# A hybrid GLA and gated-DeltaNet block on one core: where the scores, the gate and ScalarE's weight splits stand in the program order of the GDN heads

## The chip, the core and the metric

The kernel runs on one core of one Trainium2 chip. The metric is the device time of one execution in microseconds (us), lower is better; the median of three runs is given for the kernel before. Besides the times there is a profile: one execution recorded instruction by instruction.

## What is computed

One layer, 1024 tokens of width 1024, in fp32. Cut to what matters:

```python
h = rms_norm(x, pre_mix_w) * (1.0 + scale1) + shift1
proj = h @ w_in                              # q, k, v, g, ... of both branches
o_a = gla_chunked(a_q, a_k, a_v, a_gk)       # 4 heads, gated linear attention
y_a = (rms_norm(o_a, gla_onorm_w) * silu(a_g)) @ w_branch_gla
d_qkv = silu(causal_short_conv(d_qkv, gdn_conv_w))          # 4 taps
o_d = gated_delta_chunked(l2_norm(d_q), l2_norm(d_k), d_v, beta, g)   # 8 heads
y_d = (rms_norm(o_d, gdn_onorm_w) * silu(d_g)) @ w_branch_gdn
merged = sigmoid(m_a) * y_a + sigmoid(m_d) * y_d
x = x + gate1 * rms_norm(merged @ w_out, post_mix_w)
y = square(relu(h2 @ mlp_w1)) @ mlp_w2       # h2: x normed and modulated again
x = x + gate2 * rms_norm(y, post_mlp_w)
```

Inside a GDN head, over chunks of tokens: `att = q k^T * decay`, then, chunk by chunk, `v_new = u - w S`, `o = q_dec S + att v_new`, `S = dec * S + k_state^T v_new`.

## The kernel before

**Matmuls.** An fp32 operand is kept as two fp32r tiles, a rounded high part and the remainder (`hH`, `hL` of the activations, `wH`, `wL` of the weights, `oH`, `oL` of a branch's output), and a product is the sum of three: high by high, low by high, high by low. `dense_b` makes one 128x1024 tile of a projection in PSUM: eight k-steps of six matmuls of 128x512 (`dense_k`), with `tick()` behind each. Two such tiles fit in PSUM at a time (pool `pm`); the small products share four half-size buffers (`pa`).

**What sets the order.** Work beside the dense tiles is put on an agenda by step: `at(dt, fn)` means dt steps from now, and in a head `on(t, fn)` means step t of that head, counted from its first k-step. `tick()` calls what is due. While the GDN heads run, and up to the fifth tile behind them, each of TensorE, VectorE and ScalarE issues in the order in which the program was written (`InOrder` with `strict`), so the agenda is the order of each queue: an instruction that isn't ready holds everything behind it on its engine. The DMA queue of SyncE isn't held to this, and loads are issued ahead.

**A GDN head** (`gdn_head`) spans three dense tiles, 24 steps: psq (steps 0 to 7), psv (8 to 15), psg (16 to 23), for q, v and the gate g. q goes through `conv_silu` during psv: a copy and three shifted multiply-adds (`cv` with `pm`), tanh on ScalarE (`si`), and a last multiply on VectorE (`cv<-si,cv`), after which q is whole. Then `att(0)` and `att(1)` make the scores on TensorE, four matmuls of 128x128 each (`pa<-cv,kT`), and VectorE multiplies them by the decays (`attT<-pa,Dt`). `eg` (the exponential of the gates, later multiplied by q to `qd`) and `ke` (k by a decay) are loaded over all partitions from `gc_d` and `ner_d` and finished on VectorE.

The head's chain of eight chunks follows at its steps 24 to 47, in the first two tiles of the next head (head 7's in the first two tiles of the branch matmul): every three steps `c0` (transpose of v and `st,ke`, then `rs` on ScalarE), `c1` (`pa<-rs,U`, then `vn` on ScalarE) and `c2` (`vn,kt`, `vn,attT`, `st,eg`, then the new state `st` on VectorE). After the fourth and the eighth chunk ScalarE squares and copies the outputs (`ob`, `so`). At step 48 `norm` runs 14 small instructions on VectorE (a reciprocal root by Newton steps, `rsqrt`), at 50 `scale`, at 52 and 53 `fin` transposes, and the result is multiplied by the gate and stored.

The gate is made by `silu_twice(psg)`, right behind psg's last step: tanh on ScalarE (`si<-pm`) and two halves on VectorE (`si<-si,pm`). That place, where one head ends and the next begins, is called the border here.

**The branch matmul.** Behind head 7 `dense_n` makes eight tiles of o_a by `w_branch_gla`, here oa0 to oa7, and eight more by `w_branch_gdn`. The operand o_a is loaded, cast and split tile by tile (`Split`: `load`, `high` on ScalarE, `low` on VectorE) at the steps of three tables at the end of head 7. The weights are split by `conv_w_tile`: `wH` is cast on ScalarE, `wL` is written there as the negated weight, rounded the same way, and a DMA issued from GpSimd adds the whole weight onto it from DRAM, which leaves the remainder and spends no time of VectorE. `next_w` fetches the split of the next tile while the current one runs; before, both ScalarE instructions are issued at once, at the tile's start. VectorE also sums rows of the conditioning matrix (`aacc`, `ada_sum`), one every 13 steps.

In the profile nearly every instruction has line 38, that of the recording helper; they are told apart by their tiles.

Of the kernel before, what the change touches and what calls it, by code (L numbers as in the profile page):

```python
# [8 lines left out]
F32 = mybir.dt.float32  # L9
# [41 lines left out]
def block_kernel(ctx: ExitStack, tc: tile.TileContext, x, c, ada_w, ada_b, pre_mix_w, post_mix_w,  # L51
# [332 lines left out]
    plan += [(w_in, c0 + h * 128, 128, 8, E) for h in range(8) for c0, E in ((C_DQ, (1, 5) if h else (4, 6)), (C_DV, (1, 3)), (C_DG, (1, 4)))]  # L384
    plan += [(w, j * 256, 256, 8, None) for w in (w_bgla, w_bgdn) for j in range(4)]

    def conv_w_later(raw_ap, shape, dh, dl):

        w = [None, None]

        def high():
            w[0] = t4(shape, F32R, "wH", "wt")
            A.copy(w[0], raw_ap)

        def low():
            w[1] = t4(shape, F32R, "wL", "wt")
            V.tensor_tensor(w[1], raw_ap, w[0].bitcast(F32), ALU.subtract)

        at(dh, high)
        at(dl, low)  # L400
        return w

    def splits():
        early = {}

        def load(e):
            early[e] = load_raw(*plan[e][:3])

        first = next(e for e, p_ in enumerate(plan) if type(p_[4]) is tuple)
        for e, (w, c0, n, kt, E) in enumerate(plan):  # L410
            raw = early.pop(e) if e > first else load_raw(w, c0, n)
            if type(E) is tuple:
                at(E[1] + 1, lambda: load(e + 1))
                yield conv_w_later(raw, (128, 8, 128), *E)
            elif kt == 4:
                yield [conv_w_tile(raw[:, 4 * i:4 * i + 4, :], (128, 4, 256), E=E) for i in range(2)]
            else:
                for i in range(n // 128):
                    c1 = c0 + i * 128
                    src = None if E else w[:, c1:c1 + 128].rearrange("(k p) c -> p k c", p=128)  # L420
# [354 lines left out]
    def gdn_head(h):  # L775
# [3 lines left out]
        def on(t, fn):  # L779
            at(begin + t - clock[0], fn)  # L780
# [105 lines left out]
        qd = eg  # L886
        if h == 7:
            for k in range(8):
                on((8, 9, 10, 11, 18, 18, 19, 20)[k], lambda k=k: oa_s.load(k))
                on(18 + k, lambda k=k: oa_s.high(k))  # L890
                on((19, 21, 22, 23, 25, 26, 27, 29)[k], lambda k=k: oa_s.low(k))
# [34 lines left out]
        def c2(t):  # L926
# [26 lines left out]

# [7 lines left out]
        def fin(hf):  # L961
            pt, h_ = pat(), slice(hf * 512, (hf + 1) * 512)
            for i in range(4):
                t = hf * 4 + i
                T.transpose(pt[:, i * 128:(i + 1) * 128], c["ob"][:, t * 128:(t + 1) * 128], ident)
            on(53 + hf, lambda: V.scalar_tensor_tensor(sg[:, h_], pt, don, sg[:, h_], ALU.mult, ALU.mult))
            if hf:
                on(56, lambda: A.dma_start(od_d[h], sg))
# [12 lines left out]
        sg = silu_twice(psg)  # L981


    smask = [None]
# [917 lines left out]
    fin = {}  # L1902
# [72 lines left out]
```

## Time and profile before

| | |
|---|---|
| median of three runs | 1965.05 us (1964.96 to 1965.36) |
| the profiled execution's own time | 1965.17 us |
| its span | 1963.4 us, 25782 instructions |
| mean granted TensorE clock | 0.990 |
| granted clock by slices | 8 tenths in the first of 40 slices, 9 or more in all others |
| HBM traffic | 220.14 MB read, 75.15 MB written, 150 GB/s over the span |

A timeline row gives the start in us, the duration (of a group: from its first start to its last end), the engine, the operation, the tile written and the tiles read, the count, and in brackets how long the engine stood idle before it, with what ended the idle time. A windows row gives for a stretch of time each engine's busy time, then the granted clock, the DMA engines' mean share and their GB/s. A waits row gives the idle time in us, the number of waits and the longest. Durations of matmuls overlap, since they are pipelined.

### The profile page before, as it was taken

Reading aid. Unit: us, or ns where it says so; the run is one execution under the profiler, and the core shown is the slowest. Engines: PE = TensorE matmul, PEld = TensorE weight load, DVE = VectorE, ACT = ScalarE, POOL = GpSimd, SP = SyncE. Lnnn points to the kernel's source line nnn. Section 1 sums busy time; section 2 is a strip of 40 time slices with the busy share of each in tenths; the row PEclk is TensorE's granted clock in tenths of the full one; section 3 lists DMA queues with packets and bytes.
Section 4 is the critical chain, followed back from the end, with each engine's and each line's share of the span. In section 5 each row is a group of like instructions: output and inputs, shape, how many; then the busy total and the mean of one; then the engine's idle time right before and its main releaser. Section 6 shows DMA issues by size and latency. Waiting matters only on the chain.

```text
span 1963.4 us, 25782 instructions
## 1 busy us (share of the span) xinstructions
PE 1913.2 (97%) x9847; PEld 1610.1 (82%) x9847; DVE 1367.0 (70%) x2454; ACT 819.1 (42%) x1483; POOL 171.3 (9%) x120
## 2 busy tenths in 40 slices
PE   5999999999999999999999999999999999999998
PEld 4778888889899888888887888888888888888886
DVE  7866599758768556666666234666668886787887
ACT  5545322342342344444445331247644446343333
POOL 3400100310101100000000110000012220000001
PEclk8999999999999999999999999999999999999999
DMA  9355631423122434444456895244666767452525
GB/s 296 110 203 176 207 104 69 161 65 107 55 76 65 144 112 128 128 128 128 128 180 170 192 216 120 106 129 161 203 213 215 248 225 256 162 204 63 205 97 97
DMA packets 217850, 296.96 MB, mean 151 GB/s; under 512 B 36016, under 2 KB 156351, under 8 KB 217727
## 3 DMA queue, kind: packets, MB, share of 16 engines
q1 hardware_dynamic: 178238, 248.22, 39.2%
q10 hardware_dynamic: 21840, 35.04, 4.8%
q0 software_dynamic: 17648, 12.06, 4.6%
q8 instruction: 77, 1.26, 0.3%
q14 instruction: 47, 0.38, 0.1%
HBM read 220.14 MB, written 75.15 MB: 150 GB/s over the span
## 4 chain that ended last, share of the span: by engine, by line
PE 93%; DVE 2%; DMA 2%; ACT 1%; issue 1%; SPq 1%; DVEq 0%; ACTq 0%
PE pm L38 62%; PE pa L38 31%; DMA araw<-in_ada_w_dram 1%; DVE acc L38 1%; DVE cv L38 1%; DMA gr<-gc_d 1%; DMA x<-in_x_dram 0%; DVE gr L38 0%; DVE lba L38 0%; SPq L227 0%; SPq L220 0%; ACT ktok L38 0%; ACT oH L38 0%; DVE ya L38 0%; DVE rt L38 0%
## 5 line engine op out<-in xcount | busy, mean ns | idle before, releaser
L38 PE MATMUL pm<-hH,wH 128*128 128x512 f32 x1008 | 330.3, 409 | 3.8 <-DVE cv L38 3.8
L38 PE MATMUL pm<-hL,wH 128*128 128x512 f32 x1008 | 314.3, 392 | 0.0
L38 PE MATMUL pm<-hH,wL 128*128 128x512 f32 x1008 | 312.5, 391 | 0.1
L38 PEld LDWEIGHTS pm<-hH,wL 128*128 128x128 f32 x1008 | 189.4, 188 | 42.2 <-DVE wL L38 0.5
L38 PEld LDWEIGHTS pm<-hL,wH 128*128 128x128 f32 x1008 | 189.6, 188 | 41.6
L38 PE MATMUL pa<-w,yH 128*128 128x512 f32 x688 | 212.0, 389 | 0.0
L38 PEld LDWEIGHTS pm<-hH,wH 128*128 128x128 f32 x1008 | 173.1, 189 | 27.9 <-ACT gr L38 3.1
L38 ACT CAST wH<-raw 128x1024 fp32r<-128x1024 f32 x95 | 99.4, 1052 | 217.2 <-PE pm L38 131.1
L38 DVE TENSOR_TENSOR w<-raw,w 128x512 fp32r<-128x512 f32 (+1 forms) x142 | 123.6, 873 | 49.1 <-ACT w L38 48.4
L38 PEld LDWEIGHTS pa<-w,yH 128*128 128x128 f32 x688 | 129.0, 188 | 27.1 <-DVE ya L38 0.4
L38 ACT CAST w<-raw 128x512 fp32r<-128x512 f32 (+1 forms) x143 | 98.2, 709 | 88.6 <-DVE raw L38 79.5
L38 PE MATMUL pa<-w,yL 128*128 128x512 f32 x344 | 133.8, 389 | 0.0
L38 PE MATMUL pa<-oB,w 128*128 128x512 f32 x480 | 111.4, 390 | 0.0
L38 DVE SCALAR_TENSOR_TENSOR cv<-pm,ccol,cv 128x1023 f32<-128x1023 f32 (+2 forms) x72 | 92.1, 1279 | 21.2 <-ACT cv L38 19.9
L38 PEld LDWEIGHTS pa<-oB,w 128*128 128x128 f32 x480 | 89.7, 188 | 18.6 <-DVE w L38 0.2
L38 DVE TENSOR_TENSOR wL<-raw,wH 128x1024 fp32r<-128x1024 f32 x72 | 88.4, 1233 | 12.1 <-ACT wH L38 12.0
L38 PE MATMUL pm<-oT,w 128*128 128x512 f32 x384 | 90.8, 389 | 0.0
L38 PE MATMUL pa<-oT,w 128*128 128x512 f32 x384 | 90.8, 389 | 0.0
L38 DVE TENSOR_TENSOR ya<-pa,ya 128x512 f32<-128x512 f32 x82 | 55.8, 690 | 43.6 <-PE pa L38 43.6
L38 DVE SCALAR_TENSOR_TENSOR st<-st,decB,pa 128x128 f32<-128x128 f32 x48 | 16.7, 347 | 99.7 <-PE pa L38 99.6
L38 PEld LDWEIGHTS pa<-oT,w 128*128 128x128 f32 x384 | 72.1, 188 | 15.0
L38 PEld LDWEIGHTS pm<-oT,w 128*128 128x128 f32 x384 | 72.1, 188 | 15.0
(334 smaller groups left out, 3796.4 us busy)
## 6 DMA issues: line engine op xcount, KB each, us to landing
yL<-y_d SPq DMA_DIRECT2D x53, 512.0 KB
raw<-in_mlp_w_dram SPq DMA_DIRECT2D x23, 1024.0 KB
raw<-in_w_in_dram SPq DMA_DIRECT2D x19, 1024.0 KB
raw<-in_w_in_dram SPq DMA_DIRECT2D x34, 512.0 KB
araw<-in_ada_w_dram SPq DMA_DIRECT2D x32, 512.0 KB
raw<-in_mlp_w_dram SPq DMA_DIRECT2D x18, 512.0 KB
araw<-in_ada_w_dram SPq DMA_DIRECT2D x32, 256.0 KB
sg_d<-sig ACTq DMA_DIRECT2D x16, 512.0 KB
```

Source lines behind the costliest of these rows:

```text
L38: r = fn(*args, **kw)
```

## The change

All of it lies in the GDN heads and the branch matmul behind them; no instruction is added or taken away.

- The scores `att(0)`, `att(1)` move from steps 14 and 15 to 15 and 16, and the multiplies of `attT` from 15 and 16 to 16 and 17.
- The multiply of `ke` moves from step 17 to 13, that of `qd` from 16 to 15.
- The gate's tanh and its two halves move from the border to steps 26, 27 and 28 of the head, in head 7 to 29, 30 and 31.
- Squares and copy of the outputs get an agenda entry of their own; in head 6 the second four, the norm, scale, fin and the store come seven steps later (`late`).
- The splits of the branch weights are put on the agenda: `wH` one step and `wL` two steps after the fetch; for the first raw block of `w_branch_gla` at 1 and 1, then at 2 and 3.
- In head 7 the tables of o_a's loads, casts and splits change at some places.

```diff
-    def conv_w_later(raw_ap, shape, dh, dl):
+    def conv_w_later(raw_ap, shape, dh, dl, src=None):
...
         def low():
             w[1] = t4(shape, F32R, "wL", "wt")
-            V.tensor_tensor(w[1], raw_ap, w[0].bitcast(F32), ALU.subtract)
+            if src is None:
+                V.tensor_tensor(w[1], raw_ap, w[0].bitcast(F32), ALU.subtract)
+            else:
+                A.activation(w[1], raw_ap, AF.Copy, scale=-1.0)
+                G.dma_start(w[1], src, accum_op=ALU.add)
...
-                    yield conv_w_tile(raw[:, :, i * 128:(i + 1) * 128], (128, 8, 128), E=E, src=src)
+                    part = raw[:, :, i * 128:(i + 1) * 128]
+                    if E:
+                        yield conv_w_tile(part, (128, 8, 128), E=E)
+                    else:
+                        d_ = ((1, 1), (2, 3))[i] if w is w_bgla and c0 == 0 else (1, 2)
+                        yield conv_w_later(part, (128, 8, 128), *d_, src=src)
...
-            on(15 + hf, lambda: V.tensor_mul(z["att"][:, hf * 512:(hf + 1) * 512], pt, Dt[:, hf * 512:(hf + 1) * 512]))
+            on(16 + hf, lambda: V.tensor_mul(z["att"][:, hf * 512:(hf + 1) * 512], pt, Dt[:, hf * 512:(hf + 1) * 512]))
...
-                on(18 + k, lambda k=k: oa_s.high(k))
+                on((18, 19, 20, 22, 23, 24, 25, 28)[k], lambda k=k: oa_s.high(k))
...
         on(13, lambda: A.activation(eg, eg, AF.Exp))
-        on(14, lambda: att(0))
-        on(15, lambda: att(1))
+        on(13, lambda: V.tensor_tensor(ke, kT, ke, ALU.mult))
+        on(15, lambda: att(0))
+        on(16, lambda: att(1))
         on(15, squares)
-        on(16, lambda: V.tensor_tensor(qd, q, eg, ALU.mult))
-        on(17, lambda: V.tensor_tensor(ke, kT, ke, ALU.mult))
+        on(15, lambda: V.tensor_tensor(qd, q, eg, ALU.mult))
...
             if i == 3:
-                if not hf:
-                    c["ob"] = t4(p="ob")
-                for i in range(4):
-                    t_ = hf * 4 + i
-                    A.activation(c["ob"][:, t_ * 128:(t_ + 1) * 128], po[:, i * 128:(i + 1) * 128], AF.Square,
-                                 accum_out=so[:, t_:t_ + 1])
-                A.copy(c["ob"][:, hf * 512:(hf + 1) * 512], po)
+                on(47 + late if hf else 35, lambda: results(hf, po))
+
+        late = 7 if h == 6 else 0
...
-        on(48, norm)
-        on(50, scale)
-        on(52, lambda: fin(0))
-        on(53, lambda: fin(1))
+        on(48 + late, norm)
+        on(50 + late, scale)
+        on(52 + late, lambda: fin(0))
+        on(53 + late, lambda: fin(1))
         psg = dense_b(h_rhs)
 
-        sg = silu_twice(psg)
+        sg = t4(p="si")
+
+        def gate(hf):
+            h_ = slice(hf * 512, (hf + 1) * 512)
+            V.scalar_tensor_tensor(sg[:, h_], sg[:, h_], 1.0, psg[:, h_], ALU.add, ALU.mult)
+
+        g0 = 29 if h == 7 else 26
+        on(g0, lambda: A.activation(sg, psg, AF.Tanh, scale=0.5))
+        on(g0 + 1, lambda: gate(0))
+        on(g0 + 2, lambda: gate(1))
```

VectorE in head 7, around the end of psv, before: the conv's last tap, the wL of the next tile, the state st, a row sum aacc, the end of q (cv by si), and the scores.

```order
L38 TENSOR_TENSOR uw_8640<-pa_8809,nbrX 128x256
L38 TENSOR_TENSOR wL_8855<-raw_8704,wH_8797 128x1024
L38 SCALAR_TENSOR_TENSOR st_8889<-st_8828,decB,pa_8848 128x128
L38 SCALAR_TENSOR_TENSOR aacc_7985<-araw_8729,sc,aacc_7985 128x1024
L38 SCALAR_TENSOR_TENSOR cv_8767<-si_8853,cv_8767 128x1024
L38 TENSOR_TENSOR attT_8896<-pa_8897,Dt_8643 128x512
L38 TENSOR_TENSOR eg_8771<-cv_8767,eg_8771 128x1024
```

The same place now.

```order
L38 TENSOR_TENSOR uw_8637<-pa_8809,nbrX 128x256
L38 TENSOR_TENSOR wL_8855<-raw_8704,wH_8797 128x1024
L38 TENSOR_TENSOR ke_8774<-kT_8639,ke_8774 128x1024
L38 SCALAR_TENSOR_TENSOR st_8890<-st_8828,decB,pa_8848 128x128
L38 SCALAR_TENSOR_TENSOR aacc_7985<-araw_8729,sc,aacc_7985 128x1024
L38 SCALAR_TENSOR_TENSOR cv_8767<-si_8853,cv_8767 128x1024
L38 TENSOR_TENSOR eg_8771<-cv_8767,eg_8771 128x1024
L38 TENSOR_TENSOR attT_8908<-pa_8909,Dt_8640 128x512
```

ke has moved ahead of st, and qd (written over eg) ahead of attT; in heads 1 to 6 the rows are the same without aacc.

ScalarE from the border before oa0 on, before: ob and so are head 6's squares, rs and vn head 7's chain, si the gate, wH and wL the split for oa1.

```order
L38 ACTIVATE ob_8832,so_8513<-pa_8891 128x128 x4
L38 COPY ob_8832<-pa_8891 128x512
L38 CAST oH_9053<-os_8969 128x1024
L38 CAST oH_9077<-os_8988 128x1024
L38 ACTIVATE rs_9081<-pa_9079,rbC 128x128
L38 ACTIVATE si_9083<-pm_8941 128x1024
L38 CAST wH_9087<-raw_8880 128x1024
L38 ACTIVATE wL_9088<-raw_8880 128x1024
L38 CAST oH_9101<-os_9004 128x1024
L38 ACTIVATE vn_9104<-pa_9079,ksC 128x128
L38 COPY vn_9104<-pa_9079 128x128
```

Now, from the same rs on:

```order
L38 ACTIVATE rs_9060<-pa_9058,rbC 128x128
L38 CAST oH_9072<-os_8988 128x1024
L38 ACTIVATE vn_9075<-pa_9058,ksC 128x128
L38 COPY vn_9075<-pa_9058 128x128
L38 COPY st_9087<-pa_9058 128x128
L38 CAST wH_9091<-raw_8881 128x1024
L38 ACTIVATE rs_9102<-pa_9099,rbC 128x128
L38 ACTIVATE wL_9105<-raw_8881 128x1024
L38 CAST oH_9114<-os_9020 128x1024
L38 ACTIVATE vn_9121<-pa_9099,ksC 128x128
L38 COPY vn_9121<-pa_9099 128x128
L38 ACTIVATE si_9062<-pm_8936 128x1024
```

Between the first rs and its vn one cast is left; wH and wL stand one chain step later with rs between, and the gate's tanh behind the second vn, with head 6's squares yet further down.

VectorE, head 7's gate, before, at the beginning of oa0: the last rows of head 6's norm (rt, rs), both halves of head 7's gate, and what follows.

```order
L38 TENSOR_TENSOR rt_9064<-rt_9064,so_8513 128x8
L38 SCALAR_TENSOR_TENSOR rs_9063<-rt_9064,rs_9063 128x8
L38 SCALAR_TENSOR_TENSOR si_9083<-si_9083,pm_8941 128x512 x2
L38 TENSOR_TENSOR oL_9099<-os_8967,oH_9035 128x1024
L38 TENSOR_TENSOR ob_8832<-ob_8832,rs_9063 128x1024
```

Now, at the end of oa0: the first half of the gate and the first rows of the norm.

```order
L38 SCALAR_TENSOR_TENSOR si_9062<-si_9062,pm_8936 128x512
L38 TENSOR_SCALAR so_8513<-so_8513 128x8
L38 SCALAR_TENSOR_TENSOR so_8513<-vq_8355,so_8513 128x8
L38 TENSOR_SCALAR rt_9168<-so_8513 128x8
L38 TENSOR_SCALAR rs_9167<-rt_9168 128x8
```

Eight rows of the same kind follow; then come the norm's last two, the second half of the gate, the chain's st, and za, the first work on oa0's finished tile.

```order
L38 TENSOR_TENSOR rt_9168<-rt_9168,so_8513 128x8
L38 SCALAR_TENSOR_TENSOR rs_9167<-rt_9168,rs_9167 128x8
L38 SCALAR_TENSOR_TENSOR si_9062<-si_9062,pm_8936 128x512
L38 SCALAR_TENSOR_TENSOR st_9197<-st_9135,decB,pa_9148 128x128
L38 TENSOR_TENSOR za_9203<-pm_9063,sl_9201 128x1024
```

The whole norm now lies between the two halves of the gate, at the end of oa0 instead of ahead of the gate at its beginning.

More of the change, by code (lines that the diff above doesn't have):

```diff
@@ L419, in splits @@
                     c1 = c0 + i * 128
-                    src = None if E else w[:, c1:c1 + 128].rearrange("(k p) c -> p k c", p=128)
+                    src = w[:, c1:c1 + 128].rearrange("(k p) c -> p k c", p=128)
                     if i == n // 128 - 1 and e > first and e + 1 < len(plan):
                         at(4, lambda: load(e + 1))
-                    yield conv_w_tile(raw[:, :, i * 128:(i + 1) * 128], (128, 8, 128), E=E, src=src)
+                    part = raw[:, :, i * 128:(i + 1) * 128]
[4 more added lines that the diff above has]
+                        yield conv_w_later(part, (128, 8, 128), *d_, src=src)
         yield None
@@ L888, in gdn_head @@
             for k in range(8):
-                on((8, 9, 10, 11, 18, 18, 19, 20)[k], lambda k=k: oa_s.load(k))
-                on(18 + k, lambda k=k: oa_s.high(k))
-                on((19, 21, 22, 23, 25, 26, 27, 29)[k], lambda k=k: oa_s.low(k))
+                on((8, 9, 10, 11, 18, 18, 19, 21)[k], lambda k=k: oa_s.load(k))
+                on((18, 19, 20, 22, 23, 24, 25, 28)[k], lambda k=k: oa_s.high(k))
+                on((19, 20, 21, 23, 24, 25, 26, 29)[k], lambda k=k: oa_s.low(k))
         on(13, lambda: A.activation(eg, eg, AF.Exp))
-        on(14, lambda: att(0))
-        on(15, lambda: att(1))
+        on(13, lambda: V.tensor_tensor(ke, kT, ke, ALU.mult))
+        on(15, lambda: att(0))
+        on(16, lambda: att(1))
         on(15, squares)
-        on(16, lambda: V.tensor_tensor(qd, q, eg, ALU.mult))
-        on(17, lambda: V.tensor_tensor(ke, kT, ke, ALU.mult))
+        on(15, lambda: V.tensor_tensor(qd, q, eg, ALU.mult))
         on(28, lambda: token_part(0))
@@ L943, in c2, with results @@
             if i == 3:
-                if not hf:
-                    c["ob"] = t4(p="ob")
-                for i in range(4):
-                    t_ = hf * 4 + i
-                    A.activation(c["ob"][:, t_ * 128:(t_ + 1) * 128], po[:, i * 128:(i + 1) * 128], AF.Square,
-                                 accum_out=so[:, t_:t_ + 1])
-                A.copy(c["ob"][:, hf * 512:(hf + 1) * 512], po)
+                on(47 + late if hf else 35, lambda: results(hf, po))
+        late = 7 if h == 6 else 0
+        def results(hf, po):
+            if not hf:
+                c["ob"] = t4(p="ob")
+            for t in range(hf * 4, hf * 4 + 4):
+                A.activation(c["ob"][:, t * 128:(t + 1) * 128], po[:, t % 4 * 128:(t % 4 + 1) * 128], AF.Square,
+                             accum_out=so[:, t:t + 1])
+            A.copy(c["ob"][:, hf * 512:(hf + 1) * 512], po)
         def norm():
@@ L965, in fin @@
                 T.transpose(pt[:, i * 128:(i + 1) * 128], c["ob"][:, t * 128:(t + 1) * 128], ident)
-            on(53 + hf, lambda: V.scalar_tensor_tensor(sg[:, h_], pt, don, sg[:, h_], ALU.mult, ALU.mult))
+            on(53 + late + hf, lambda: V.scalar_tensor_tensor(sg[:, h_], pt, don, sg[:, h_], ALU.mult, ALU.mult))
             if hf:
-                on(56, lambda: A.dma_start(od_d[h], sg))
+                on(56 + late, lambda: A.dma_start(od_d[h], sg))
                 dump("odT", sg, lambda t: t[h * 128:(h + 1) * 128, :])
```

## Prediction

> **What bounds the kernel now.** I read the page's first part first. TensorE is the engine that counts: all others are far from full.
>
> ```profile
> PE 1913.2 (97%) x9847; PEld 1610.1 (82%) x9847; DVE 1367.0 (70%) x2454; ACT 819.1 (42%) x1483; POOL 171.3 (9%) x120
> ```
>
> Only what lets PE idle, or slows its clock, can be won back. So I asked the waits view for PE from 690 to 1110 us, the stretch of the eight GDN heads and the first tiles of the branch matmul behind them, where every edit of the change lies.
>
> ```profile
> PE pa L38 <- issue: 9.4, 7, 2.4
> PE pa L38 <- ACT vn L38: 2.3, 1, 2.3
> PE pa L38 <- ACT rs L38: 0.6, 1, 0.6
> PE pm L38 <- DMA wL<-in_w_branch_gla_dram: 0.3, 1, 0.3
> ```
>
> That is all of it: 12.6 us. Seven waits have no releaser named ("issue"); to find the cause I put PE's timeline beside VectorE's in head 1. First PE: the last matmul of the chain's step (st,eg), the scores att(0) (cv,kT), a k-step of the dense tile (pm, three rows to the next), the next chain step (ident,cv), the scores att(1), and where psg begins.
>
> ```profile
> 735.48 0.39 PE L38 MATMUL pa<-st,eg 128*128 128x128 f32 x2
> 737.04 1.13 PE L38 MATMUL pa<-cv,kT 128*128 128x128 f32 x8 [1.18 <-issue]
> 737.93 0.71 PE L38 MATMUL pm<-hH,wH 128*128 128x512 f32 x2
> ...
> 739.41 0.27 PE L38 MATMUL pa<-ident,cv 128*128 128x128 f32 x1
> ...
> 739.74 0.50 PE L38 MATMUL pa<-cv,kT 128*128 128x128 f32 x3
> ...
> 742.15 0.70 PE L38 MATMUL pm<-hH,wH 128*128 128x512 f32 x2
> ```
>
> Then VectorE: the wL before it, the chain's state st, and the multiply that finishes q.
>
> ```profile
> 731.05 1.22 DVE L38 TENSOR_TENSOR wL<-raw,wH 128x1024 fp32r<-128x1024 f32 x1
> 735.46 0.35 DVE L38 SCALAR_TENSOR_TENSOR st<-st,decB,pa 128x128 f32<-128x128 f32 x1 [3.19 <-PE pa L38]
> 735.72 1.22 DVE L38 SCALAR_TENSOR_TENSOR cv<-si,cv 128x1024 f32<-128x1024 f32 x1
> ```
>
> q is done at 735.72 + 1.22 = 736.94, and att(0), which reads it, starts 0.10 us later. Head 7 shows the same with one more instruction (aacc) between, and a longer wait:
>
> ```profile
> 1027.65 0.39 PE L38 MATMUL pa<-st,eg 128*128 128x128 f32 x2
> 1030.41 1.13 PE L38 MATMUL pa<-cv,kT 128*128 128x128 f32 x8 [2.37 <-issue]
> ...
> 1037.09 0.71 PE L38 MATMUL pm<-hH,wH 128*128 128x512 f32 x2
> ```
>
> ```profile
> 1027.89 1.28 DVE L38 SCALAR_TENSOR_TENSOR aacc<-araw,sc,aacc 128x1024 f32<-128x1024 f32 x1
> 1029.09 1.22 DVE L38 SCALAR_TENSOR_TENSOR cv<-si,cv 128x1024 f32<-128x1024 f32 x1
> ```
>
> Here q is done at 1030.31, and PE again starts 0.10 later. From att(0) to psg head 7 takes 1037.09 - 1030.41 = 6.68 us, head 1 takes 742.15 - 737.04 = 5.11: behind the long wait another 1.57 us are lost. Windows show the clock: 1.00 around a 1.18 us wait of head 1, and under 1 for three windows behind the 2.28 us wait of the tail (the granted clock is the column before the DMA share).
>
> ```profile
> 730.00:740.00 10.00, 8.82 (x64) 7.41 (x63) 6.74 (x8) 5.00 (x16) 0.00 (x0) 1.00 0.28 70
> ...
> 1058.00:1060.00 2.00, 1.88 (x8) 1.60 (x9) 2.00 (x3) 0.33 (x2) 0.57 (x1) 0.71 0.85 293
> 1060.00:1062.00 2.00, 2.00 (x8) 1.61 (x7) 2.00 (x3) 0.04 (x1) 0.00 (x0) 0.50 1.09 378
> 1062.00:1064.00 2.00, 2.00 (x13) 1.63 (x12) 1.97 (x3) 0.33 (x1) 0.00 (x0) 0.94 1.17 230
> ```
>
> So a wait of 2.3 us costs itself and a slow clock, one of 1.2 us only itself.
>
> **The tail** is the first branch tile, oa0; here are the starts of oa0 and oa1, the first use of oa1's low weights, and the start of oa2.
>
> ```profile
> 1051.20 0.71 PE L38 MATMUL pm<-oH,wH 128*128 128x512 f32 x2
> ...
> 1072.04 0.71 PE L38 MATMUL pm<-oH,wH 128*128 128x512 f32 x2
> ...
> 1073.05 0.62 PE L38 MATMUL pm<-oH,wL 128*128 128x512 f32 x2
> ...
> 1086.18 0.71 PE L38 MATMUL pm<-oH,wH 128*128 128x512 f32 x2
> ```
>
> oa0 takes 20.84 us, oa1 14.14. ScalarE's timeline tells why: between two steps of the chain stand squares, casts, the gate's tanh (si) and a split (wH, wL), and vn, which PE needs, comes last.
>
> ```profile
> 1049.98 0.28 ACT L38 ACTIVATE ob<-pa 128x128 f32<-128x128 f32 x1
> ...
> 1051.64 1.99 ACT L38 CAST oH<-os 128x1024 fp32r<-128x1024 f32 x2
> ...
> 1053.79 1.02 ACT L38 ACTIVATE si<-pm 128x1024 f32<-128x1024 f32 x1
> 1054.70 1.05 ACT L38 CAST wH<-raw 128x1024 fp32r<-128x1024 f32 x1
> 1055.63 1.07 ACT L38 ACTIVATE wL<-raw 128x1024 fp32r<-128x1024 f32 x1
> ...
> 1057.53 0.38 ACT L38 ACTIVATE vn<-pa,ksC 128x128 f32<-128x128 f32 x1
> ```
>
> The three waits are 0.3 + 0.6 + 2.3 us. The slow clock behind costs at least 2 x (0.29 + 0.50 + 0.06) = 1.7 us by the windows; at most what is left of 20.84 - 14.14 - 3.1 = 3.6, which also holds head 6's eight transposes of fin, work that stays. I take 2.4.
>
> **The change part by part.** The numbers of instructions stay the same; each edit only moves.
>
> *Scores a step later (heads 0 to 7).* att(0) now stands behind one more k-step and one chain step. Without its wait the k-step would start at 737.04 - 1.18 = 735.86; k-step and chain step take 739.41 - 737.93 = 1.48 and 739.74 - 739.41 = 0.33, so att(0) is wanted at 737.67, and may start at 737.04: covered by 0.6 us. The six waits of heads 1 to 6 go: 9.4 - 2.37 = 7.0 us. What would be late next is the multiply of att, which nobody needs before the next tile. In head 7 aacc still stands between: the k-step would start at 1030.41 - 2.37 = 1028.04, att(0) is wanted 1.81 later, at 1029.85, and possible at 1030.41: 0.6 us remain, too short for the clock, so 2.37 + 1.57 - 0.6 = 3.3 us go.
>
> *ke ahead of st, qd ahead of attT.* ke (1.22 us by its like, wL) now stands on VectorE behind wL and ahead of st; it fits the 3.19 us that VectorE idles there, if its loads have landed (a rival, below). It leaves the place behind st and eases psg's taps. qd now runs ahead of attT; its first user is the chain's second step, over a tile away. Nothing for both.
>
> *The gate's tanh off the border.* In heads 0 to 6 no wait of PE stands at a border, so nothing is won; psg's buffer is held some three steps longer, but is wanted only at the tile after the next, 8 steps off. In the tail it helps: tanh, wH and wL leave the queue ahead of vn, so the waits of 0.6 and 2.3 us go and with them the 2.4 us of slow clock: 5.3 us. The first wait, 0.3 us, is for oa0's own wL, which ScalarE and GpSimd issue in the same place as before: it stays.
>
> *Results and norm of head 6 seven steps later, gate of head 7 at steps 5 to 7 of oa0.* Now one buffer does bind: oa1 writes where psg stood, and must wait for the gate's second half on VectorE, which stands behind the whole norm of head 6.
>
> ```profile
> 1051.15 0.18 DVE L38 TENSOR_SCALAR so<-so 128x8 f32<-128x8 f32 x1
> ...
> 1053.59 0.17 DVE L38 SCALAR_TENSOR_TENSOR rs<-rt,rs 128x8 f32<-128x8 f32 x1
> 1054.85 1.28 DVE L38 SCALAR_TENSOR_TENSOR si<-si,pm 128x512 f32<-128x512 f32 x2 [1.09 <-ACT si L38]
> ```
>
> By before's clock: a step of oa takes 14.14 / 8 = 1.77. The squares come at step 6, 1051.20 + 6 x 1.77 = 1061.8, behind the chain's matmuls and rs (0.7 as an estimate from the 0.33 chain step and vn's 0.38), and take 1.17 (1049.98 to the norm's start at 1051.15): 1063.7. The norm takes 1053.59 + 0.17 - 1051.15 = 2.6, half a gate 0.64: 1066.9. oa1 is wanted at 1051.20 + 14.14 = 1065.3. So up to 1.6 us of new wait; I take 1.3 (0 to 1.6), since the steps of oa0 are rather longer.
>
> *ScalarE's splits dealt out.* oa1's wL is now written after step 3: 1051.20 + 5.3 + 0.7 + 1.07, so GpSimd issues it at about 1058.3, 1.3 us later than before, while PE wants it some 4 us earlier. Before, it was issued at 1057.02 and took 12.1 us; the next tile's took 7.6 (the last number of the DMA rows):
>
> ```profile
> 1057.02 1.56 POOL L38 DMA_DIRECT2D wL<-in_w_branch_gla_dram  x1 [14.11 <-ACT wL L38]
> ```
> ```profile
> wL<-in_w_branch_gla_dram POOLq DMA_DIRECT2D x1, 512.0 KB, 12.1
> ```
> ```profile
> wL<-in_w_branch_gla_dram POOLq DMA_DIRECT2D x1, 512.0 KB, 7.6
> ```
>
> It lands between 1065.9 and 1070.4, in the middle 1068.1. It is wanted 1073.05 - 1072.04 = 1.0 after oa1's start, and with the gate's wait that is 1067.6: 0.5 us late, 0 to 2.8. The later tiles' splits move by up to two steps; their rows wait nowhere now. I take 0.3 for them, as the one such wait costs today, and 0 to 1.5.
>
> The Trainium skill would make this term vanish: DMA: Bandwidth & Descriptors, Anatomy of one DMA, gives a DMA issued from GpSimd about 2.0 us and its bytes at 436 GB/s, an estimate of 3.2 us for 512 KB, and a sum lower by 0.8. The trace disagrees (7.6 and 12.1 us), and the sum goes by the trace.
>
> **The sum**, against the profiled execution of 1965.17 us (span 1963.4): heads 7.0 + 3.3 = 10.3; tail 5.3 - 1.3 - 0.5 - 0.3 = 3.2; together 13.5. That gives 1951.7, and as the median shown lies 0.12 lower, 1951.5. Its own range: 1948.6 (every new wait nought and fin's part small: 16.5 won) to 1953.6.
>
> **The rivals.** *The tail only trades its waits.* The wL of oa1 takes 12.1 us again and is 2.8 late; a wait over 2.3 us draws a slow clock behind it, 1.7 us or more. The tail then gives 5.3 - 1.3 - 2.8 - 1.7 - 0.3 = -0.8, and the time is 1955.5; with later tiles late too, 1957.0. For it: the one landing in just this place took 12.1. Chance 0.24.
>
> *The slow stretches don't come from the waits.* The 1.57 and 2.4 us stay though the waits go: 1951.5 + 4.0 = 1955.5. Against it: clock 1.00 beside short waits, and both drops right behind long ones. Chance 0.05. The Trainium skill leans to this one: TensorE: Matmul & The Clock Gate, The HAM clock gate, has the clock halved after an idle window of about 3.4 us, longer than any wait here. The trace disagrees as far as it goes: 0.50 was granted behind 2.28 us.
>
> *The scores wait as before.* "issue" names no releaser; if the 0.10 us is chance and something on PE's own queue holds att, the wait moves along with it. Heads give nothing: 1961.9; with half, 1956.7. Chance 0.10.
>
> *Slower: ke's load.* On VectorE's queue st, q and attT stand behind ke, and behind st PE's chain. Head 1's load of ke:
>
> ```profile
> 714.56 0.73 SPq L885 DMA_DIRECT2D ke<-ner_d  x1
> ```
>
> ke's turn comes at 731.05 + 1.22 = 732.27, 17.7 us after that; 3.19 - 1.22 = 2.0 us more are free, and 0.6 behind. A load that lands later than 20.3 us after its issue stalls PE in each head, and from 2.3 us of stall on with 1.6 of slow clock: seven heads at 3.9 are 27, less 13.5 won: about 1979. To end slower at all takes 13.5 + 3.9 = 17.4, or 2.5 a head. Against it: the DMA engines were busy for 0.28 of 730 to 740, so nothing queues there. Chance 0.03.
>
> **How the numbers follow.** Forecast 0.58, the others 0.24, 0.05, 0.10, 0.03. The range runs from 1948.6 to 1957.0: it takes in the first two rivals and leaves out most of the third and the last. A measurement of this kernel tells about 0.2%, 3.9 us, from no change: up to 1961.1 is faster. That is all but the worst of the third rival (0.03) and the last (0.03).
>
> **What would show it.** Right: no wait ahead of cv,kT in heads 1 to 6, some 0.6 us in head 7, clock 1.00 behind it; vn's wait gone from oa0; one wait of about 1 us at oa1's first matmul, released by VectorE's gate, and a short one for wL. Wrong: waits that follow att to its new place, waits of st for ke, or a clock of 0.5 in oa1.

## The result, and the profile after

The changed kernel takes 1950.54 us in the median of four runs (1946.63 to 1953.06), the kernel before 1965.2 us (four runs, 1964.96 to 1966.17). The ratio is 0.9923, with a 95% interval of 0.9904 to 0.9942: faster by some 15 us (11 to 19 by the interval). Forecast was 1951.5. The sum came out within a us; its terms did not all, as shown below.

The profiled execution of the changed kernel takes 1948.84 us (span 1947.1), 16.3 less than that of before. The waits of PE from 680 to 1110 us are now these (idle time, number, longest):

```profile
PE pm L38 <- DMA wL<-in_w_branch_gla_dram: 1.3, 2, 0.8
PE pm L38 <- DVE si L38: 0.9, 1, 0.9
PE pa L38 <- ACT rs L38: 0.7, 1, 0.7
```

The seven waits without a releaser and those for vn and, in the tail, for rs are gone; the forecast ones for the gate (si) and for wL are there, and one of 0.7 us in head 7 that the profile puts down to ScalarE's rs. To see where the time went I put the same instruction of both runs side by side: the first step of the chain in head 0 (vn,kt), before and after. What the change touches ahead of it lies in head 0, and PE waits there in neither profile.

```profile
711.87 0.38 PE L38 MATMUL pa<-vn,kt 128*128 128x128 f32 x2
```
```profile
708.55 0.38 PE L38 MATMUL pa<-vn,kt 128*128 128x128 f32 x2
```

So 3.3 of the 16.3 us lie in the start of the kernel. They are there already ahead of every GDN head, where the same group of PE starts at 528.02 us before and at 524.70 after, so the change didn't make them; over all profiles of this study that row stands between 708.5 and 712.7. The other 13.0 us come out of three stretches, measured from start to start of the same PE instruction:

| stretch | before | after | difference |
|---|---|---|---|
| head 1 to head 7's last chain step before its scores | 292.17 | 283.54 | -8.63 |
| head 7, the step with the scores | 11.35 | 8.06 | -3.29 |
| from there to oa0 | 12.64 | 12.62 | 0.0 |
| oa0 | 20.84 | 15.59 | -5.25 |
| oa1 | 14.14 | 17.62 | +3.48 |
| from oa0 to the end of the span, oa0 and oa1 included | 912.2 | 911.2 | -1.0 |

Head 6's fin, some 0.9 us of transposes, now lies in oa1 and no longer in oa0: without any wait the two take 14.5 and 15.0 us (e3 and e7, below).

**Heads 1 to 6** give 8.63 / 6 = 1.44 each, more than the 1.18 us of idle time that the waits view showed. Head 1 of after tells why: st,eg, the k-step that now follows it, the scores, and psg.

```profile
732.16 0.39 PE L38 MATMUL pa<-st,eg 128*128 128x128 f32 x2
732.30 0.71 PE L38 MATMUL pm<-hH,wH 128*128 128x512 f32 x2
...
734.10 1.06 PE L38 MATMUL pa<-cv,kT 128*128 128x128 f32 x8
...
737.41 0.71 PE L38 MATMUL pm<-hH,wH 128*128 128x512 f32 x2
```

From st,eg to psg it is 5.25 us, before 742.15 - 735.48 = 6.67. Where nothing is awaited the next matmul starts 0.14 us after the start of st,eg; with the wait it started 1.56 later, and only the part behind the recorded end of the pair st,eg (0.39) counts as idle. A wait of PE costs its idle time and some 0.24 us more (0.22 to 0.29 in the stretches below).

**Head 7** keeps a wait; VectorE's rows stand under PE's.

```profile
1018.46 1.13 PE L38 MATMUL pa<-cv,kT 128*128 128x128 f32 x8 [0.65 <-ACT rs L38]
```
```profile
1015.94 1.28 DVE L38 SCALAR_TENSOR_TENSOR aacc<-araw,sc,aacc 128x1024 f32<-128x1024 f32 x1
1017.14 1.22 DVE L38 SCALAR_TENSOR_TENSOR cv<-si,cv 128x1024 f32<-128x1024 f32 x1
```

q is done at 1018.36 and att(0) starts 0.10 later, as in every head before: the wait is for q, whatever releaser is named.

**The tail.** ScalarE is free again between rs and vn, with one cast between, and vn waits for PE:

```profile
1036.29 0.37 ACT L38 ACTIVATE rs<-pa,rbC 128x128 f32<-128x128 f32 x1
1036.55 1.05 ACT L38 CAST oH<-os 128x1024 fp32r<-128x1024 f32 x1
1037.82 0.37 ACT L38 ACTIVATE vn<-pa,ksC 128x128 f32<-128x128 f32 x1 [0.22 <-PE pa L38]
```

At the start of oa1 stand the two new waits, for the gate and for wL (by starts the first still counts into oa0's stretch); VectorE's rows show the gate's half right behind the norm.

```profile
1051.53 0.73 PE L38 MATMUL pm<-oH,wH 128*128 128x512 f32 x2 [0.89 <-DVE si L38]
1052.10 0.62 PE L38 MATMUL pm<-oL,wH 128*128 128x512 f32 x2
1053.49 1.22 PE L38 MATMUL pm<-oH,wL 128*128 128x512 f32 x2 [0.76 <-DMA wL<-in_w_branch_gla_dram]
```
```profile
1048.29 0.17 DVE L38 TENSOR_SCALAR so<-so 128x8 f32<-128x8 f32 x1 [1.21 <-ACT ob L38]
...
1050.71 0.17 DVE L38 SCALAR_TENSOR_TENSOR rs<-rt,rs 128x8 f32<-128x8 f32 x1
1050.80 0.68 DVE L38 SCALAR_TENSOR_TENSOR si<-si,pm 128x512 f32<-128x512 f32 x1
```

And behind two waits of under 1 us the granted clock (the column before the DMA share) fell all the same:

```profile
1052.00:1054.00 2.00, 1.24 (x5) 0.75 (x4) 2.00 (x3) 0.00 (x0) 0.00 (x0) 0.88 0.41 50
1054.00:1056.00 2.00, 2.00 (x7) 1.52 (x6) 0.56 (x5) 0.61 (x2) 0.00 (x0) 0.50 0.68 242
1056.00:1058.00 2.00, 2.00 (x9) 1.67 (x8) 0.00 (x0) 0.92 (x2) 0.00 (x0) 0.77 0.00 0
```

### The profile page after: what moved, and what is told of

Its sections match the earlier page's. It is cut to its first block, busy times and chain, and to the rows that moved or that the text cites. A ratio compares the mean times of both kernels' runs of the same rounds, so it can differ in the third digit from the quotient of the medians.

```text
span 1947.1 us, 25780 instructions
## 1 busy us (share of the span) xinstructions
PE 1910.8 (98%) x9847; PEld 1609.0 (83%) x9847; DVE 1367.2 (70%) x2454; ACT 819.2 (42%) x1483; POOL 170.9 (9%) x120
## 3 DMA queue, kind: packets, MB, share of 16 engines
q8 instruction: 77, 1.26, 0.3%
## 4 chain that ended last, share of the span: by engine, by line
PE 92%; DMA 3%; DVE 2%; issue 2%; SPq 1%; ACT 0%; POOL 0%; DVEq 0%; ACTq 0%; POOLq 0%
PE pm L38 61%; PE pa L38 31%; DMA araw<-in_ada_w_dram 1%; DVE acc L38 1%; DMA wL<-in_w_branch_gla_dram 1%; DMA x<-in_x_dram 1%; DVE cv L38 0%; DMA dec_d<-dec 0%; DMA gr<-gc_d 0%; DVE lba L38 0%; SPq L227 0%; DVE gr L38 0%; SPq L220 0%; POOL wL L38 0%; ACT ktok L38 0%
## 5 line engine op out<-in xcount | busy, mean ns | idle before, releaser
L38 DVE TENSOR_TENSOR wL<-raw,wH 128x1024 fp32r<-128x1024 f32 x72 | 88.3, 1231 | 11.8 <-ACT wH L38 11.7
L38 PE MATMUL pm<-oH,wH 128*128 128x512 f32 x256 | 82.0, 402 | 0.9 <-DVE si L38 0.9
```

Source lines behind the costliest of these rows:

```text
L38: r = fn(*args, **kw)
```

## The experiments

The stretches of each kernel's profile, in us, from start to start as above; the last column is from oa0 to the end of the span. The start of the kernel is left out of them, and so is its scatter. "Heads" is the first row of the table above, "head 7" the second. The profiled execution of e6 was granted a clock of 0.95 where the others had 1.00; the stretches in which nothing differs are up to 0.2% longer there, as are its heads (284.06).

| kernel | heads | head 7 | oa0 | oa1 | to the end |
|---|---|---|---|---|---|
| before | 292.17 | 11.35 | 20.84 | 14.14 | 912.2 |
| changed | 283.54 | 8.06 | 15.59 | 17.62 | 911.2 |
| changed, again (a1) | 283.54 | 8.06 | 15.62 | 16.24 | 910.0 |
| scores alone (e1) | 283.54 | 8.06 | 20.87 | 14.10 | 912.2 |
| all but the scores (e2) | 292.15 | 11.37 | 15.62 | 15.09 | 909.1 |
| gate at the border (e6) | 284.06 | 8.09 | 14.55 | 16.09 | 909.6 |
| splits at once (e7) | 283.54 | 8.06 | 16.63 | 15.01 | 909.1 |
| norm a step later (e3) | 283.54 | 8.06 | 14.48 | 17.83 | 911.0 |
| the same again (e13) | 285.13 | 8.06 | 14.48 | 18.61 | 911.8 |
| oa1's wL earlier (e4) | 283.54 | 8.06 | 15.58 | 15.99 | 910.3 |
| oa1's wL later, norm later (e12) | 283.54 | 8.06 | 14.48 | 17.39 | 910.9 |
| four edits (e9) | 283.54 | 7.17 | 14.43 | 16.16 | 908.0 |
| e9 with the raw load behind wL (e10) | 283.54 | 7.17 | 14.43 | 16.04 | 907.8 |
| splits at once, norm later (e11) | 283.54 | 8.07 | 15.49 | 16.00 | 909.1 |

### The scores alone, and all but the scores

```diff
 # on the kernel before
-            on(15 + hf, lambda: V.tensor_mul(z["att"][:, hf * 512:(hf + 1) * 512], pt, Dt[:, hf * 512:(hf + 1) * 512]))
+            on(16 + hf, lambda: V.tensor_mul(z["att"][:, hf * 512:(hf + 1) * 512], pt, Dt[:, hf * 512:(hf + 1) * 512]))
...
-        on(14, lambda: att(0))
-        on(15, lambda: att(1))
+        on(15, lambda: att(0))
+        on(16, lambda: att(1))
```

> The kernel before with the scores and the multiplies of attT one step later, and nothing else of the change. Theory (the scores stood ahead of the end of q): the six waits of 1.2 us of heads 1 to 6 go, 7.0 us; in head 7 the wait falls from 2.4 to about 0.6 us and the slow clock behind it goes, 3.3 us; the tail keeps its waits of 0.3, 0.6 and 2.3 us and its slow clock: about 1954.9. Rival 1 (the new places of ke and qd free VectorE, and the scores alone only carry their wait along): within 2 us of 1965. Rival 2 (the slow clock does not come from the waits): 1956.5, with a clock of 0.5 still in head 7.

Measured: 1952.97 us (1951.11 to 1955.07), before on the same chip 1965.3 (1961.27 to 1967.0); ratio 0.9948 (0.9932 to 0.9964). Its waits:

```profile
PE pa L38 <- ACT vn L38: 2.3, 1, 2.3
PE pa L38 <- ACT rs L38: 1.1, 2, 0.7
PE pm L38 <- DMA wL<-in_w_branch_gla_dram: 0.4, 1, 0.4
```

The heads take the same time as in the whole change, to the hundredth, and the tail the same as before. So the scores' step gives the whole gain of the heads, 11.9 us, and ke and qd give nothing: rival 1 falls. Head 7 takes 8.06 us without its long wait, so the slow clock went with it: rival 2 falls too. The gain is above the theory's 10.3, by the 0.24 us a wait.

The other way about, the changed kernel with the same lines taken back:

> The changed kernel with the scores and the multiplies of attT back at their old steps. Theory: all seven waits come back ahead of the scores, 1.2 us in heads 1 to 6 and 2.4 us with a slow clock in head 7, and the tail keeps its gain: 10.3 us over the changed kernel, about 1961. Rival 1 (ke and qd are what helps): 1951 to 1953.

Measured: 1962.53 us (1959.92 to 1965.66), ratio 0.9994 (0.9985 to 1.0004), which can't be told from no change by the runs. The waits are back, and the eighth, 0.30 us, is for head 0's scores:

```profile
PE pa L38 <- issue: 9.7, 8, 2.4
PE pm L38 <- DVE si L38: 0.9, 1, 0.9
PE pm L38 <- DMA wL<-in_w_branch_gla_dram: 0.8, 1, 0.8
```

The heads are those of before; by the stretches the tail alone gives 912.2 - 909.1 = 3.1 us. Its wait for the gate is as in the changed kernel, but the one for wL stands at oa3, and oa1 takes 15.09 us where the changed kernel took 17.62: here wL landed after 9.5 us instead of 10.4 and was in time at oa1, and the clock stayed.

### What cleared the tail

The gate back at the border, the rest as changed:

```diff
-        g0 = 29 if h == 7 else 26
-        on(g0, lambda: A.activation(sg, psg, AF.Tanh, scale=0.5))
-        on(g0 + 1, lambda: gate(0))
-        on(g0 + 2, lambda: gate(1))
+        A.activation(sg, psg, AF.Tanh, scale=0.5)
+        gate(0)
+        gate(1)
```

> The changed kernel with the gate's tanh and halves back at the border in every head. Theory (ScalarE's queue between rs and vn is the sum of what stands there): at the border before oa0 tanh and one cast stand there, 2.1 us less than before, so the wait for vn is 0.2 us instead of 2.3; at the start of oa1 the wait for the gate, 0.9 us, is gone and that for wL grows by as much: 1949 to 1951. Rival (the gate alone filled the border): waits of 2 us and a slow clock in oa0 again, 1954 to 1956.

Measured: 1950.33 us (1947.3 to 1952.6). oa0 takes 14.55 us, so nothing of it waits at the border, and nothing for the gate; wL is 0.8 us late at oa1 and 1.25 at oa3.

The splits at once again, the rest as changed:

```diff
-                    if E:
-                        yield conv_w_tile(part, (128, 8, 128), E=E)
+                    if 1:
+                        yield conv_w_tile(part, (128, 8, 128), E=E, src=None if E else src)
```

> The changed kernel with ScalarE's splits of the branch weights issued at once again, at the start of each tile. Theory: at the start of oa0 wH and wL, 2.1 us, stand ahead of vn again, a wait of about 1.2 us there, too short for the clock; GpSimd gets oa1's wL some 2 us earlier, so the wait for it at oa1 is gone and that for the gate stays: 1949 to 1951. Rival (the splits alone filled the border): waits of 2 us and a slow clock in oa0 again, 1954 to 1956.

Measured: 1950.39 us (1947.62 to 1951.08). The waits:

```profile
PE pm L38 <- DVE si L38: 0.9, 1, 0.9
PE pa L38 <- ACT vn L38: 0.8, 1, 0.8
PE pa L38 <- ACT rs L38: 0.7, 1, 0.7
```

The waits for vn came out at nought and 0.8 us, where the theory's sum of ScalarE's queue had 0.2 and 1.2: it is that sum, and neither edit's work alone, that held vn up. The wait for rs, 0.6 us before, stays away in both; whether head 6's squares or o_a's casts, which also moved, had caused it was not tried. And either edit alone leaves the tail no longer than both, 909.6 and 909.1 against 911.2 and 910.0: the second edit gained nothing here, because the waits at oa1 came in its place.

### The gate's wait and wL's

The changed kernel once more, unchanged:

> The changed kernel once more, for the scatter of its start and of its tail. Theory (two short waits within 2 us of each other at oa1 let the clock fall): the heads take the same time to 0.1 us, oa1 has waits of 0.9 us for the gate and 0.5 to 1.5 us for wL; where both come, oa1 takes about 17.6 us, where wL is in time about 15. Rival (the slow clock of oa1 was chance): oa1 near 15.8 us with both waits and a clock of 1.00.

Measured: 1948.92 us (1947.48 to 1951.41). The same two waits, 0.89 and 0.94 us:

```profile
1055.30 0.73 PE L38 MATMUL pm<-oH,wH 128*128 128x512 f32 x2 [0.89 <-DVE si L38]
1057.44 0.74 PE L38 MATMUL pm<-oH,wL 128*128 128x512 f32 x2 [0.94 <-DMA wL<-in_w_branch_gla_dram]
```
```profile
1056.00:1058.00 2.00, 1.06 (x5) 0.49 (x4) 1.99 (x4) 0.00 (x0) 0.00 (x0) 1.00 0.29 47
1058.00:1060.00 2.00, 2.00 (x13) 1.72 (x12) 0.34 (x2) 1.30 (x2) 0.00 (x0) 1.00 0.57 229
```

The clock stayed at 1.00. The theory that two short waits as such bring it down falls: with waits as long, it fell in one profile and not in the other (more under The clock).

The norm one step later, so that the gate's second half runs ahead of it:

```diff
-        late = 7 if h == 6 else 0
+        late = 8 if h == 6 else 0
```

> The changed kernel with head 6's squares, norm, scale and fin one step later (late = 8), so that the gate's second half runs ahead of the norm. Theory: the wait for the gate at oa1, 0.9 us, goes, and the wait for wL, which it covered, grows by as much, to some 1.7 us, in one piece; if the clock stays, oa1 takes 15.8 us, if it falls as behind 2.3 us, 17.5: no gain from the edit by itself, 1949 to 1952. Rival (the gate is the cause and wL comes in time): oa1 at 14.2 us with no wait.

Measured: 1951.33 us (1948.03 to 1955.21). oa0 falls to 14.48 us, and the wait for wL comes out from behind the gate's, in one piece of 2.58 us, longer than the 1.7 expected; no gain, as expected. But the clock stayed at 1.00 behind the longest wait of the study:

```profile
1058.04 0.74 PE L38 MATMUL pm<-oH,wL 128*128 128x512 f32 x2 [2.58 <-DMA wL<-in_w_branch_gla_dram]
```
```profile
1058.00:1060.00 2.00, 1.96 (x10) 1.64 (x11) 1.67 (x4) 0.85 (x2) 0.00 (x0) 1.00 0.55 172
```

oa1's wL two steps earlier:

```diff
-                        d_ = ((1, 1), (2, 3))[i] if w is w_bgla and c0 == 0 else (1, 2)
+                        d_ = ((1, 1), (1, 1))[i] if w is w_bgla and c0 == 0 else (1, 2)
```

> The changed kernel with oa1's split at steps 1 and 1 instead of 2 and 3, so that GpSimd issues its wL some 2 us earlier. Theory: the wait for wL at oa1 goes, the wait of 0.9 us for the gate stays and the clock stays at 1.00: oa1 takes 15.0 us instead of 17.6, the whole 2.5 us less than the changed kernel: about 1948. Rival 1 (the landing is set by the other DMAs and not by the issue): the wait for wL stays at 0.8 us. Rival 2 (the gate's wait alone lets the clock fall): oa1 at 16.7 us.

Measured: 1950.14 us (1949.58 to 1952.08). Rival 1 holds: GpSimd issued it 4.6 us after oa0's start instead of 7.1, 2.4 us sooner, and it was 0.70 us late all the same, with a landing of 12.8 us. SyncE's row beside GpSimd's shows a 1 MB load that goes out in the same moment, since the split frees its buffer:

```profile
1044.44 0.38 SPq L175 DMA_DIRECT2D raw<-in_w_branch_gla_dram  x1
```
```profile
1044.72 1.55 POOL L38 DMA_DIRECT2D wL<-in_w_branch_gla_dram  x1 [13.78 <-ACT st L38]
```
```profile
wL<-in_w_branch_gla_dram POOLq DMA_DIRECT2D x1, 512.0 KB, 12.8
```

### All of it mended, and what came next

Four edits on the changed kernel: every later split at steps 1 and 1, the norm a step later, and the one aacc of head 7 a step earlier.

```diff
-                        d_ = ((1, 1), (2, 3))[i] if w is w_bgla and c0 == 0 else (1, 2)
+                        d_ = (1, 1)
...
-        late = 7 if h == 6 else 0
+        late = 8 if h == 6 else 0
...
-        at(2 + 13 * n, lambda n=n: ada_rest(n))
+        at(2 + 13 * n - (n == 28), lambda n=n: ada_rest(n))
```

> The changed kernel with every later split of the branch weights at steps 1 and 1, head 6's norm one step later, and the one aacc of head 7 that stood between st and the end of q issued a step earlier. Theory: no wait of PE is left between 690 and 1110 us; head 7's last 0.65 us, the gate's 0.9, wL's 0.8 and 0.5 and the slow clock of oa1 go: from oa0 to the end 909.1 - 0.9 = 908.2 us, and some 4.5 us less than the changed kernel, about 1946. Rival (the waits move on to the next tiles or to vn): waits of 1 us or more in oa0 to oa3, no gain.

Measured: 1948.24 us (1945.99 to 1950.22); ratio 0.9921 (0.9906 to 0.9936), the changed kernel on the same chip 0.9922 (0.9906 to 0.9939). The tail takes 908.0 us, near the 908.2 expected, but by another way, since one wait stayed; head 7's wait is gone and took 0.89 us with it, its idle 0.65 and 0.24 more. One wait is left, against the theory:

```profile
1054.12 0.73 PE L38 MATMUL pm<-oH,wL 128*128 128x512 f32 x2 [0.88 <-DMA wL<-in_w_branch_gla_dram]
```

So the next kernel holds the 1 MB load back, by issuing it from ScalarE's queue, which keeps the program's order:

```diff
-            early[e] = load_raw(*plan[e][:3])
+            late_q = plan[e][0] is w_bgla and plan[e][1] > 0
+            early[e] = load_w(*plan[e][:3], q=A) if late_q else load_raw(*plan[e][:3])
```

> The kernel with all four edits, and the 1 MB loads of the next raw blocks of w_branch_gla issued from ScalarE's queue at their step instead of from SyncE's, where they went out as soon as a buffer came free, in the same moment as oa1's wL. Theory (oa1's wL is late because that load runs beside it, not because of its own issue): wL lands some 8 us after its issue instead of 11.8, the last wait of 0.9 us goes, oa1 takes 15.0 us and the time from oa0 to the end is 906.9. Rival 1 (GpSimd's DMA with an addition is slow by itself, or other loads slow it): landing 11 us or more, oa1 at 16.1. Rival 2 (the raw block now comes late itself): a wait for wL at oa2.

Measured: 1946.98 us (1945.68 to 1947.52); ratio 0.9916 (0.9901 to 0.9931). The load now goes out 2.4 us behind wL, and wL lands after 8.4 us instead of 11.8:

```profile
1045.11 0.43 ACTq L38 DMA_DIRECT2D raw<-in_w_branch_gla_dram  x1
```
```profile
wL<-in_w_branch_gla_dram POOLq DMA_DIRECT2D x1, 512.0 KB, 8.4
```

The wait for wL is gone: at this place the load beside it made the difference. But oa1 still takes 16.04 us and the tail 907.8, not the 15.0 and 906.9 expected; the norm now stands ahead of the chain's state st, and PE waits for that:

```profile
1054.99 0.49 PE L38 MATMUL pa<-st,ke 128*128 128x128 f32 x2 [0.76 <-DVE st L38]
```
```profile
1052.08 0.17 DVE L38 TENSOR_SCALAR so<-so 128x8 f32<-128x8 f32 x1 [2.49 <-ACT ob L38]
...
1054.51 0.17 DVE L38 SCALAR_TENSOR_TENSOR rs<-rt,rs 128x8 f32<-128x8 f32 x1
1054.59 0.34 DVE L38 SCALAR_TENSOR_TENSOR st<-st,decB,pa 128x128 f32<-128x128 f32 x1
```

The splits at once with the norm a step later end in the same place:

> The changed kernel with the splits issued at once again and head 6's norm one step later. Theory (each wait costs its idle time and 0.24 us more, and the gate waits only because the norm stands between its halves): of the waits of 0.8 us for vn and 0.9 us for the gate in oa0 only the first stays, oa0 takes 15.5 us instead of 16.6, oa1 15.0, and from oa0 to the end 908.0. Rival (the wait for wL comes out from behind the gate's, as it did with the norm alone a step later): oa1 at 16 us or more and no gain.

Measured: 1949.76 us (1949.22 to 1950.08). oa0 takes 15.49 us as expected and wL is in time, but the same wait of 0.77 us for st at oa1 takes the gain back. The gate's wait and this one have one cause, 14 small instructions of 2.6 us in a row on VectorE between two things that PE needs.

e10 has the lowest median of the study, 1.9 us under the changed kernel's in the series before; by the runs the two can't be told apart (0.9916 and 0.9922). By the stretches, it is shorter by 910.0 - 907.8 = 2.2 us behind oa0's start and 0.9 in head 7.

### The clock

oa1's wL issued later still, with the norm later, one profile:

```diff
-                        d_ = ((1, 1), (2, 3))[i] if w is w_bgla and c0 == 0 else (1, 2)
+                        d_ = ((1, 1), (3, 4))[i] if w is w_bgla and c0 == 0 else (1, 2)
```

> The changed kernel with the norm one step later and oa1's split at steps 3 and 4, so that its wL is issued some 2 us later still. Theory: one wait for wL of about 4 us at oa1; what is asked is the clock behind it. If the length of a wait decides, the clock falls and oa1 takes 15.0 + 4 + 0.24 + 1.6 = 20.9 us; if 2.6 us left it at 1.00 because the clock doesn't follow waits at all, 19.3.

Measured: 1950.61 us. It missed its aim: wL landed in 8.4 us, although the 1 MB load moved along with the split and still went out 0.3 us ahead, and the wait was 2.16 us, not 4. The clock stayed at 1.00.

And the kernel with the norm later, a second time:

> The changed kernel with the norm one step later, a second time: one wait of about 2.6 us for wL at oa1. If the length decides, the clock stays at 1.00 as in its first profile and oa1 takes 17.8 us; if it is the moment at which the wait falls, it may as well drop to 0.5, and oa1 takes 19.4.

Measured: 1955.05 us. The wait was shorter than in the first profile, 1.77 us, and the clock fell:

```profile
1058.00:1060.00 2.00, 1.13 (x6) 0.99 (x7) 1.96 (x7) 0.00 (x0) 0.00 (x0) 0.89 0.04 5
1060.00:1062.00 2.00, 2.00 (x6) 1.61 (x6) 1.34 (x2) 1.30 (x2) 0.00 (x0) 0.50 0.74 231
1062.00:1064.00 2.00, 2.00 (x9) 1.63 (x9) 0.00 (x0) 0.83 (x3) 0.00 (x0) 0.75 0.08 31
```

So it isn't the length: 2.58 us left it alone, 1.77 us brought it down, in one and the same kernel. The same run lost another 1.59 us in the heads, in a place where no wait stands: sixteen matmuls of one column, and a clock of 0.50 behind them.

```profile
906.12 1.95 PE L38 MATMUL pa<-onesR,aacc 128*128 128x1 f32 x16
...
909.91 1.20 PE L38 MATMUL pm<-hH,wH 128*128 128x512 f32 x2
```
```profile
910.00:912.00 2.00, 2.00 (x7) 1.61 (x6) 1.97 (x5) 0.37 (x1) 0.00 (x0) 0.50 0.00 0
```

What sets the waits apart is where they fall. In each of the 14 profiles all times at which the granted clock changes lie on a grid with steps of 3.41 us, which stands differently against the kernel from run to run, and each fall between 690 and 1110 us lasts one step: 3.41 us at half the clock, 1.7 us by this reckoning, 1.6 as measured. Windows cut at this grid, for PE alone (length, PE's busy time, granted clock, DMA share, GB/s), show the changed kernel with its two waits in one step, and the clock in the next:

```profile
1050.09:1053.50 3.41, 1.76 (x10) 1.00 0.85 107
1053.50:1056.91 3.41, 3.41 (x10) 0.50 0.50 154
```

And e3, where a step's end cuts the wait of 2.58 us in two:

```profile
1053.40:1056.81 3.41, 2.06 (x14) 1.00 0.59 79
1056.81:1060.23 3.42, 2.19 (x11) 1.00 0.42 133
```

So PE idled 1.65 us of one step in the first, 1.35 and 1.23 of two in the second. In a1 the two waits lie in two steps (0.89 and 0.94), e12's 2.16 us are cut into 1.04 and 1.12, and e13's 1.77 lie in one. Between 690 and 1110 us of all 14 profiles every step with 1.65 us or more of PE idle was followed by a fall, and none with 1.35 or less but the one with the one-column matmuls. The limit itself stays open: near 80 and 110 us, ahead of the heads, steps with 1.8 to 1.9 us of idle kept the clock. So do the one-column matmuls: in e6 and e9 all sixteen lie in one step as well, and the clock stayed.

## Why the prediction was right, and where it wasn't

**The heads: mechanism right, size too small.** "The scores stood ahead of the end of q" is shown by e1 and e2. The term "9.4 - 2.37 = 7.0 us" measured 8.63: the waits view gives idle time behind the recorded end of the last matmul, and each wait costs 0.24 us more than that. Head 7 came out as forecast, 3.29 for 3.3, the remaining wait 0.65 for 0.6 (its cost is 0.89, as e9 shows). In heads 1 to 6 the scores now start 0.48 us behind the end of q, near the 0.6 reckoned.

**ke ahead of st.** Nothing for nothing, as forecast; no wait for ke or its load appears in any run. The rival that ends slower is refuted, the one in which the wait moves along with the scores too.

**The tail: the waits right, their sum too good.** Forecast was 3.2 us; the profiles give 1.0, and 2.2 on repetition (3.1 in e2, where wL came in time at oa1). The term of 2.4 us for the slow clock behind vn fits in size, but is two things: a fall of 1.6 us and 0.24 us for each of three waits (oa0's 20.84 less 14.5 without waits, 0.9 for fin and 3.1 of waits leaves 2.3). The border cleared as said, and more, since oa0's own wait for wL, which I had kept, went as well. The gate's wait came out at 0.89 (1.3 forecast), that for oa1's wL at 0.76 and 0.94 (0.5), the later ones at 0.52 and 0.55 (0.3), and each with 0.24 on top: 2.9 to 3.1 us in place of 2.1. In the first profile the clock fell too, 1.6 us. That is the failing step: "a wait of 2.3 us costs itself and a slow clock, one of 1.2 us only itself" was read from too few waits, each priced by itself, while the runs show the idle time of one step of the clock's grid added up: 0.89 and 0.76 us in one step brought a fall, 2.58 us in two did not. The first rival, the tail that only trades its waits, thus came in about half, without its long landing.

The Trainium skill (TensorE: Matmul & The Clock Gate, The HAM clock gate) has the clock set by how busy the PE was in a free-running window of about 3.4 us, so that where work falls in the window matters. That agrees with the runs: the clock changes on a grid of 3.41 us, and equal waits come with and without a fall by where its steps cut them. Its rule that an idle window of about 3.4 us is needed doesn't: 1.65 us of one step was enough. This rests on waits that happened to fall one way or the other; no run moved a wait against the grid on purpose, and the fall behind matmuls of one column stays unexplained.

**GpSimd's wL.** I took the middle of two landings, 9.8 us; it took 10.4 and 10.6. e10 against e9 shows what the 1 MB load that the split itself sets free does to it: 8.4 us with that load 2.4 us behind, 11.8 with it ahead by 0.3. But e12 has 8.4 with it ahead by 0.3 too, so it isn't that load alone. What SyncE's queue moved in all while wL was under way goes with the landing: nothing at oa2's wL of the changed kernel (6.2 us), 1.05 MB in e12 (8.4), 1.26 in the changed kernel (10.4), 1.91 in e9 (11.8), 1.95 in e4 (12.8). An earlier split moves the 1 MB load along and meets more of the loads issued before, so issuing wL 2.4 us sooner had it land at most 0.3 us sooner (e4).

**The total** of 1951.5 fits the median of 1950.54 in part by luck, because two errors cancel: the heads gave 1.6 us more, the tail 1.0 to 2.2 less. The profile pair alone would mislead, since 3.3 of its 16.3 us are the scatter of the start.

## What to carry to other kernels

In a queue held to program order, look for the instruction that stands one place ahead of its own input, and move it behind other work: here three lines gave 11.9 of 13 to 14 us, and the rest of a long change gave 1 to 3. When a wait is cleared, ask what else the step brings along (here a load for the buffer it frees) and what stands next in the same row, since waits that were cleared in the tail kept uncovering others. And compare start to start of the same instruction in two profiles, stretch by stretch: idle time understates a wait, and totals hold the scatter of stretches that nothing changed.

## What the runs showed of the hardware that was not expected

- A wait of PE costs its recorded idle time and about 0.24 us: behind a pair of 128x128 matmuls the next starts 0.14 us after the pair's start, while the pair's record lasts 0.39.
- The granted clock fell behind waits of 2.37, 2.28 and 1.77 us and behind 0.89 and 0.76 together, and did not behind 2.58, 2.16, and 0.89 and 0.94 together. It changes only on a grid of 3.41 us, and PE's idle time within one step of it tells them apart: 1.65 us or more with a fall, 1.35 or less without, between 690 and 1110 us. A fall lasts one step and costs 1.6 us. It also fell once behind sixteen one-column matmuls without a wait.
- A granted clock of 0.95 over the whole execution (e6) made the stretches at most 0.2% longer.
- A 512 KB DMA from GpSimd that adds onto its target landed after 6.0 us at the least, and in oa0 after 12.8 with 1.95 MB of SyncE's queue moved meanwhile.
- A releaser named by the profile can be one that had long been done: head 7's wait for q is put down to ScalarE's rs.
